# A hybrid diffusion backbone in fp32: each engine's instructions taken from a list schedule of the whole program

## The chip, the cores and the metric

The kernel runs on one core of a Trainium2 chip. The metric is device time in microseconds (us), the median of several runs. A core has five instruction streams that run side by side and each in its own order: TensorE (PE, matmuls; PEld is its weight load), VectorE (DVE), ScalarE (ACT), GpSimd (POOL) and SyncE (SP, which here only issues transfers). An instruction starts when its engine has started all those ahead of it and when the semaphores that it waits on have come; so the order inside each stream decides what stands behind a wait.

## The reference

The reference is a two-layer backbone over 256 context tokens and 512 latent tokens of width 1024, in fp32. Cut to what matters here, one layer is:

```python
p = modulate(x, sh1, sc1) @ w_in                     # norm(x) * (1 + sc) + sh, latent and context apart
ya = chunk_token_mlp(p[..., :512])                   # gelu, norm, 128x128 token mixing, gate
yb = gqa_mixer(p[..., 512:1152])                     # 6 query heads, 2 key heads, rotary, softmax
yc = deltanet_mixer(p[..., 1152:])                   # short conv, 6 heads, chunks of 64, both directions
x = layer_norm(ALPHA * x + g1 * (concat(ya, yb, yc) @ w_out))
m = jnp.square(jax.nn.relu(modulate(x, sh2, sc2) @ w_up)) @ w_down      # 1024 -> 4096 -> 1024
x = layer_norm(ALPHA * x + g2 * m)
```

The six modulation vectors of a layer come from `silu(c) @ mod_w`. In the second layer only the 512 latent tokens pass beyond the mixers. The gated DeltaNet is a recurrence: each chunk of 64 tokens solves a triangular system, and a 64x64 state per head passes from chunk to chunk.

## The kernel before, in words

**Arithmetic.** A large product is three matmuls of a rounded type, fp32r (`mm3`): each operand is split into a high part (a copy on ACT: `whi`, `xh`, `hh`) and a low part (a subtraction on DVE: `wlo`, `xl`, `hl`), and hi*hi, lo*hi and hi*lo are summed in PSUM. Small products and the recurrence are fp32 matmuls, which the trace records as two passes each.

**Memory.** Weights come in 512 KB pieces through `Feed` (L235): raw buffers `wraw`, filled by SP, and parts `whi` and `wlo`. PSUM is split into four slots of 512 columns (`mm`) and two of 1024 (`ax`).

**Stages**, each with its place in the profiled execution. Start (0 to 84 us): modulation of layer 0 (`modw` pieces times `cz`), norms and transposes of `xt`, first input projections (`w_ta`). Mixer input (`mix`, L711; 84 to 310 us): projections for gMLP, conv, q, k, v and z, and `dn_prep` of head pairs 0 and 1, whose triangular inverse is a chain of short DVE steps (`tm`, `Xx`), two DVE transposes (`PA`, `PB`) and 32x32 matmuls (`PB,M`; `PA,zs`). DeltaNet and attention (310 to 535): per head pair `dn_make` (`kv`, `rwu`), the state chain `dn_scan` (L1542: `S`, `rP`, `rQ`), and between them `attention` (L1056): scores into an `ax` slot (`akh,qs`), row maximum `anm` on DVE, exponential `ape` on ACT, scaling on DVE, transposes (`c_ident,ape`), copies `apT` on ACT and `att_out` (L1114), the product with the values (`apT,ava`), 64 columns of the array wide and 12 matmuls to a pair of heads. Output projection (535 to 605), then the MLP (`mlp`, L1711; 616 to 1180): eight groups of up units, each a pass over all tokens, and after each group the down product, token by token, each token in one `ax` slot whose sum DVE adds to `acc`. Layer 1 is the same with 4 token tiles in place of 6 behind the mixers: 1180 to 1424, 1424 to 1605, 1605 to 1675, 1675 to 2027. At the end each of four tokens has a norm (`acc`, `st`, `mv`, `rs`, `rstd`, twice `xt`) and a store.

**What sets the order.** `Flow` (L40) runs the stages as generators and picks, by a rough clock of its own, which one goes on next; its picks are the written order. Every instruction passes `_Engine.call`, so that all rows of the trace carry that line:

```python
def call(*args, **kw):
    self.flow.note(self.key, op, args, kw)
    return f(*args, **kw)          # L213
```

The framework then orders each engine by priority, which is the written order but for `prep`, started 300 places ahead (`AHEAD`). An accumulation group (the matmuls that sum into one slot) is written as one run, and so is each token of the down product and each pair's 12 products with the values.

Of the kernel before, what the change touches and what calls it, by code (L numbers as in the profile page):

```python
# [9 lines left out]
F32R = mybir.dt.float32r  # L10
# [3 lines left out]
PSUM = bass.MemoryType.PSUM  # L14
DRAM = bass.MemoryType.DRAM

P = 128
# [22 lines left out]
class Flow:  # L40
# [8 lines left out]
    def __init__(self, tc):  # L49
        self.tc = tc  # L50
        self.free = {}
        self.ready = {}
        self.done = {}
        self.live = []
        self.count = 0
        self.last = 0.0
        self.slots = {}
        self.spare = {}
        self.lent = {}
# [7 lines left out]
    @staticmethod  # L67
    def width(a):
        n = 1
        for s in a.shape[1:]:  # L70
            n *= s
        return n
# [150 lines left out]
            setattr(self, k, _Engine(flow, k, getattr(nc, k)))  # L223


def _tb(v):

    return 1 - v if v < 2 else 7 - v
# [62 lines left out]
class K:  # L291
    def __init__(self, ctx, tc, d, dump=None):
        self.tc = tc
        self.flow = Flow(tc)
        self.nc = _Core(tc.nc, self.flow)
        self.d = d
        self.dump = dump
        self.ctx = ctx
        self.open_ = []


    def open(self, name, side="left", space=None):
        kw = {} if space is None else {"space": space}
        cm = self.tc.tile_pool(name=name, bufs=1, side=side, reuse_waits="tile", **kw)
        p = cm.__enter__()
        self.open_.append((p, cm))
        return p

    def close(self, *pools):
        for p in pools:  # L310
            i = next(i for i, (q, _) in enumerate(self.open_) if q is p)
            self.open_.pop(i)[1].__exit__(None, None, None)

    def setup(self):
        nc, tc, ctx, d = self.nc, self.tc, self.ctx, self.d
# [348 lines left out]
def _body(ctx, tc, d, out, dump=None, stop=None):  # L664
    K_ = Kernel(ctx, tc, d, dump)
    K_.run(out, stop)
    for p, cm in reversed(K_.open_):
        cm.__exit__(None, None, None)

# [17 lines left out]
class Kernel(K):  # L687
# [784 lines left out]
    def dn_make(self, l, p, v, qkv, G, A, TT, r):  # L1472
# [5 lines left out]
        kds, ks, egc, be, E = G["kds"], G["ks"], G["egc"], G["be"], G["E"]  # L1478
        hs = slice(2 * p, 2 * p + 2)
        td = (v, _tb(v))  # L1480
        a0 = 0 if l == 0 else 2
        he = lambda a: a.rearrange("p t (h e) -> p t h e", e=HD)
# [59 lines left out]
    def dn_scan(self, l, p, v, A, r, S, o):  # L1542

        nc, sc = self.nc, self.dn
        need = l == 0 or v > 1
        a0 = 0 if l == 0 else 2
        td = (v, _tb(v))
        mm = nc.tensor.matmul
        halves = [_half(f) for f in range(2)]
# [405 lines left out]
```

## Time and profile before

| | |
|---|---|
| median of 3 runs | 2039.75 us (2034.57 to 2040.4) |
| profiled execution | 2039.17 us, span 2037.4 us, mean granted clock 0.95 |
| busy share | PE 91%, PEld 75%, DVE 63%, ACT 42%, POOL 14% |
| chain that ended last | PE 61%, DVE 18%, issue 7%, ACT 5%, POOL 4%, DMA 3% |

The busy share of PE counts matmuls that overlap in the pipeline, so a stage with a PE busy share of 80% can still have room; idle time of PE is stage length less busy time. The granted clock is 1 where TensorE runs at 2.4 GHz and 0.5 where it runs at 1.2 GHz; a stage's mean between the two tells how much of it ran at the lower level.

### The profile page before, as it was taken

The numbers are of one execution on the slowest core, as the hardware profiler recorded it, in microseconds if no ns is written. First come the engines' busy times: TensorE is split into PE (matmuls) and PEld (weight loads), VectorE is DVE, ScalarE is ACT, GpSimd is POOL, SyncE is SP. The second block draws the span as 40 slices with busy tenths as digits, with TensorE's granted clock in tenths as the row PEclk, the third lists the DMA queues.
The fourth block names the chain that finished last, engine by engine and source line by source line (L and its number), as shares of the span: only waits on it lengthen the run. The fifth ranks groups of instructions, "written<-read, shape, count | busy, mean of one in ns | idle before, by whom it ended". The sixth has DMA issues, their size and how long they took to land.

```text
span 2037.4 us, 35195 instructions
## 1 busy us (share of the span) xinstructions
PE 1859.2 (91%) x14496; PEld 1519.5 (75%) x14496; DVE 1284.2 (63%) x2165; ACT 854.5 (42%) x1607; POOL 279.2 (14%) x479
## 2 busy tenths in 40 slices
PE   6999887898898999999999989988778879999997
PEld 2778675566678878888888777877666668888886
DVE  4668786765587245464457776888785575544555
ACT  3434435456546322322232274443655545323331
POOL 1111215431021000000000111111522020000001
PEclk8989889989999999999999979987997989999999
DMA  8211015313326323242355242100000544322331
GB/s 284 93 58 50 27 37 175 120 31 118 107 96 226 99 83 115 83 155 74 113 165 185 84 147 89 62 29 21 27 27 6 189 164 136 103 83 83 114 104 52
DMA packets 74060, 204.44 MB, mean 100 GB/s; under 512 B 9730, under 2 KB 23938, under 8 KB 73900
## 3 DMA queue, kind: packets, MB, share of 16 engines
q1 hardware_dynamic: 62764, 184.51, 27.9%
q10 hardware_dynamic: 11136, 17.70, 2.3%
q8 instruction: 113, 1.85, 0.4%
q14 instruction: 47, 0.39, 0.1%
HBM read 184.38 MB, written 17.79 MB: 99 GB/s over the span
## 4 chain that ended last, share of the span: by engine, by line
PE 61%; DVE 18%; issue 7%; ACT 5%; POOL 4%; DMA 3%; SPq 0%; ACTq 0%; POOLq 0%; DVEq 0%
PE mm L213 37%; PE ax L213 25%; DVE cacc L213 2%; DVE Xx L213 2%; DVE tm L213 2%; DVE wlo L213 2%; POOL crn L213 2%; DVE M L213 1%; DMA wraw<-in_w_up 1%; POOL rs L213 1%; DVE anm L213 1%; ACT ape L213 1%; DVE st L213 1%; POOL arn L213 1%; ACT osq L213 1%
## 5 line engine op out<-in xcount | busy, mean ns | idle before, releaser
L213 ACT ACTIVATE whi<-wraw 128x1024 fp32r<-128x1024 f32 (+2 forms) x188 | 194.6, 1050 | 443.1 <-PE ax L213 287.7
L213 DVE TENSOR_TENSOR wlo<-wraw,whi 128x1024 fp32r<-128x1024 f32 (+2 forms) x188 | 226.6, 1212 | 236.5 <-ACT whi L213 235.7
L213 PE MATMUL mm<-x2xh,whi 128*128 128x256 f32 (+1 forms) x832 | 287.7, 346 | 12.3 <-ACT whi L213 11.2
L213 PE MATMUL mm<-x2xl,whi 128*128 128x256 f32 (+1 forms) x832 | 287.0, 345 | 0.0
L213 PE MATMUL mm<-x2xh,wlo 128*128 128x256 f32 (+1 forms) x832 | 285.4, 343 | 0.7 <-DVE wlo L213 0.7
L213 PE MATMUL ax<-whi,hh 128*128 128x512 f32 x640 | 251.4, 393 | 0.1
L213 PE MATMUL ax<-wlo,hh 128*128 128x512 f32 x640 | 250.2, 391 | 0.0
L213 PE MATMUL ax<-whi,hl 128*128 128x512 f32 x640 | 250.1, 391 | 0.0
L213 PEld LDWEIGHTS mm<-x2xh,whi 128*128 128x128 f32 x832 | 159.7, 192 | 34.6 <-ACT whi L213 12.0
L213 DVE TENSOR_TENSOR acc<-acc,ax 128x1024 f32<-128x1024 f32 x68 | 83.0, 1220 | 148.3 <-PE ax L213 148.2
L213 PEld LDWEIGHTS mm<-x2xh,wlo 128*128 128x128 f32 x832 | 159.0, 191 | 20.0 <-DVE wlo L213 1.1
L213 PEld LDWEIGHTS mm<-x2xl,whi 128*128 128x128 f32 x832 | 159.7, 192 | 17.5
L213 PEld LDWEIGHTS ax<-whi,hh 128*128 128x128 f32 x640 | 120.2, 188 | 29.6 <-ACT hh L213 5.6
L213 PEld LDWEIGHTS ax<-whi,hl 128*128 128x128 f32 x640 | 120.2, 188 | 27.3 <-DVE hl L213 2.9
L213 PEld LDWEIGHTS ax<-wlo,hh 128*128 128x128 f32 x640 | 120.3, 188 | 26.9 <-issue 2.6
L213 POOL TENSOR_SCALAR rs<-mv 128x1 f32<-128x1 f32 x52 | 33.1, 638 | 702.6 <-DVE mv L213 701.4
L213 DVE SCALAR_TENSOR_TENSOR acc<-modw,cz,acc 128x1024 f32<-128x1024 f32 x80 | 101.2, 1282 | 7.6 <-DMA acc<-in_mod_b 4.6
L213 ACT ACTIVATE rl<-mm 128x256 f32<-128x256 f32 (+1 forms) x104 | 50.7, 490 | 131.4 <-PE mm L213 131.4
L213 POOL MEMSET acc<- 128x1024 f32 x10 | 9.5, 955 | 468.9 <-PE mm L213 468.9
L213 DVE TENSOR_TENSOR hl<-rl,hh 128x768 fp32r<-128x768 f32 (+2 forms) x76 | 54.5, 717 | 29.7 <-ACT hh L213 29.7
L213 DVE TENSOR_REDUCE anm<-ax 128x1 f32<-128x768 f32 (+1 forms) x60 | 50.6, 848 | 33.3 <-PE ax L213 33.2
L213 DVE SCALAR_TENSOR_TENSOR cacc<-cb,cw,cacc 128x772 f32<-128x772 f32 (+1 forms) x72 | 70.0, 975 | 0.7 <-ACT cacc L213 0.2
(255 smaller groups left out, 4127.1 us busy)
## 6 DMA issues: line engine op xcount, KB each, us to landing
modw<-in_mod_w SPq DMA_DIRECT2D x80, 512.0 KB
wraw<-in_w_up SPq DMA_DIRECT2D x64, 512.0 KB
wraw<-in_w_down SPq DMA_DIRECT2D x64, 512.0 KB
wraw<-in_w_ch SPq DMA_DIRECT2D x22, 512.0 KB
modw<-in_mod_w SPq DMA_DIRECT2D x32, 256.0 KB
wraw<-in_w_out SPq DMA_DIRECT2D x16, 512.0 KB
x_d<-xt ACTq DMA_DIRECT2D x16, 512.0 KB
xt<-x_d SPq DMA_DIRECT2D x14, 512.0 KB
```

The source lines that it names most:

```text
L213: return f(*args, **kw)
```

## The change

After all instructions are written, a new class `Order` builds a graph of the whole program: which instruction reads or writes what another wrote (`graph`), which waits for a buffer of a pool to come free, and the order of first use of the buffers of a tag. `tail` gives each instruction the length of the longest chain of work from it to the end of the program. `schedule` then runs through the program with five engines and one transfer bus, always giving a free engine the ready instruction with the longest chain behind it, and `apply` fixes the resulting order of each engine with dependencies that carry no semaphore. The instructions are the same. Pools are wrapped so that their opening, closing and tiles are recorded (`Pools`, `_Pool`, not shown).

```diff
+class Order:
+    SAME, OTHER = 110.0, 220.0
...
+    def costs(self):
...
+            elif kind == "InstMatmult":
+                n = width(x.outs[0])
+                m = width(x.ins[1])
+                if x.ins[1].dtype == F32R:
+                    c = max(35.0 + 0.58 * m, 0.4175 * n + 13.0)
+                else:
+                    c = (1.0 if x.is_transpose else 2.0) * max(0.42 * m, 0.835 * n + 2.0)
+                o, l = x.outs[0].bass_ap, x.ins[1].bass_ap
+                self.cells[-1] = self.place(x)
...
+    def lag(self, i, j):
+        if i >= self.n or j >= self.n:
+            return 0.0
+        if self.moved[i]:
+            return 0.0
+        if self.eng[i] == self.eng[j]:
+            return 0.0 if self.cells[i] else self.SAME
+        return self.OTHER
...
+    def tail(self):
...
+        for i in reversed(order):
+            c = self.dur[i] + (2200.0 + self.moved[i] / 340.0 if self.moved[i] else 0.0) if i < self.n else 0.0
+            far[i] = c + max((far[j] + self.lag(i, j) for j in succ[i]), default=0.0)
+            if i < self.n:
+                far[i] = max([far[i]] + [far[j] + 1.0 for j in self.after[i]])
...
+    def schedule(self, key):
...
+        for _ in range(self.n):
+            best = None
+            for e in self.engines:
+                if avail[e]:
+                    t = free[e]
+                elif soon[e]:
+                    t = max(free[e], soon[e][0][0])
+                else:
+                    continue
+                if best is None or t < best[0]:
+                    best = (t, e)
+            t, e = best
+            while soon[e] and soon[e][0][0] <= t + 1.0:
+                r, i = heapq.heappop(soon[e])
+                heapq.heappush(avail[e], (key[i], i))
+            k, i = heapq.heappop(avail[e])
+            t = max(t, ready[i])
+            if self.cells[i]:
+                t = max([t] + [cell[c] for c in self.cells[i]])
+                for c in self.cells[i]:
+                    cell[c] = t + self.dur[i]
+                fin = t + self.dur[i]
+                free[e] = t + 7.0
+                if len(self.cells[i]) == 16:
+                    free[e] = fin
...
+    def apply(self):
+        far = self.tail()
+        out = self.schedule([-f for f in far])
+        dep = mybir.DependencyInfo(mybir.DependencyClass.NoSync, mybir.DependencyReason.DATA)
+        for e, seq in out.items():
+            for a, b in zip(seq, seq[1:]):
+                self.tc.add_manual_dep(self.ins[b], self.ins[a].name, dep)
...
 def _body(ctx, tc, d, out, dump=None, stop=None):
     K_ = Kernel(ctx, tc, d, dump)
     K_.run(out, stop)
+    Order(tc, K_.pools).apply()
```

The order that comes out stands near the written one: a matmul moves by 22 places of 11,078 on average, a DVE instruction by 7. Three places show what moves.

DVE at the end of layer 0's mixer input, where the DeltaNet begins: `PA` and `PB` close the triangular inverse of pair 1, `M` belongs to pair 2 and follows a transfer (`gc_d`), `zth` is the gate of z, `akl` the low part of the keys, and `kv` the first step of pair 0's `dn_make`. Before:

```order
L213 STREAM_TRANSPOSE PA<-Xx 128x32x32
L213 STREAM_TRANSPOSE PB<-Xx 128x32x32
L213 SCALAR_TENSOR_TENSOR zth<-zth,mm_69 128x384
L213 SCALAR_TENSOR_TENSOR zth<-zth,ng 128x384
L213 TENSOR_TENSOR M<-M,gc 128x768
L213 TENSOR_TENSOR M<-M,c_mask 128x768
L213 SCALAR_TENSOR_TENSOR zth<-zth,mm_66 128x384
L213 TENSOR_TENSOR akl<-akT,akh 64x256
L213 SCALAR_TENSOR_TENSOR zth<-zth,ng 128x384
L213 TENSOR_TENSOR akl<-akT,akh 64x256 x3
L213 TENSOR_TENSOR akl<-akT,akh 64x512 x3
L213 TENSOR_TENSOR kv<-qkv_991,ks 128x2x64 x2
```

Now:

```order
L213 TENSOR_TENSOR akl<-akT,akh 64x512
L213 TENSOR_TENSOR Xx<-Xx,tm 128x2x30
L213 TENSOR_TENSOR kv<-qkv_991,ks 128x2x64
L213 TENSOR_TENSOR tm<-Lx,Xx 128x31
L213 TENSOR_TENSOR kv<-qkv_991,ks 128x2x64
L213 TENSOR_TENSOR Xx<-Xx,tm 128x31
L213 TENSOR_TENSOR kv<-qkv_991,be 128x2x64
L213 STREAM_TRANSPOSE PA<-Xx 128x32x32
L213 STREAM_TRANSPOSE PB<-Xx 128x32x32
L213 TENSOR_TENSOR kv<-qkv_992,ks 128x2x64 x2
L213 TENSOR_TENSOR kv<-qkv_992,be 128x2x64
L213 TENSOR_TENSOR rP_2759<-mm_69,ei 128x256
```

The three `kv` of the first block stand among the last steps of the inverse and ahead of `PA` and `PB`, and `M` is no longer ahead of them. On PE the rest of pair 1's preparation (`PB,M`, `PA,zs`), which stood ahead of the last projection, now follows the first `kv,TT` and its successors.

PE in the last third of layer 0's attention, where the DeltaNet has ended; `mm` is a slot of 512 columns, `ax` one of 1024. Before:

```order
L213 MATMUL mm_69<-c_ident,ape 128x128 x4
L213 MATMUL mm_66<-c_ident,ape 128x128 x2
L213 MATMUL ax_71<-akh,qs 128x512
L213 MATMUL ax_71<-akl,qs 128x512
L213 MATMUL ax_71<-akh,qs 128x256
L213 MATMUL ax_71<-akl,qs 128x256
L213 MATMUL mm_68<-apT,ava 64x128 x11
L213 MATMUL mm_67<-c_ident,ape 128x128 x4
L213 MATMUL mm_69<-c_ident,ape 128x128 x2
```

Now:

```order
L213 MATMUL ax_70<-akh,qs 128x256
L213 MATMUL mm_68<-apT,ava 64x128 x2
L213 MATMUL ax_70<-akl,qs 128x256
L213 MATMUL mm_68<-apT,ava 64x128 x2
L213 MATMUL mm_67<-c_ident,ape 128x128
L213 MATMUL mm_68<-apT,ava 64x128 x2
L213 MATMUL mm_67<-c_ident,ape 128x128
L213 MATMUL mm_68<-apT,ava 64x128 x2
L213 MATMUL mm_67<-c_ident,ape 128x128
L213 MATMUL mm_68<-apT,ava 64x128 x2
L213 MATMUL mm_66<-c_ident,ape 128x128
L213 MATMUL mm_68<-apT,ava 64x128
```

The run of 12 products with the values is cut into pieces of one or two, and the transposes of the next heads, which stood behind it in runs of four and two, stand singly between the pieces; the scores of both following heads stand ahead.

DVE at the very end of the program, the last two tokens. Before:

```order
L213 TENSOR_TENSOR acc<-acc,ax_71 128x1024
L213 BN_STATS st<-acc 128x6 x2
L213 BN_AGGR mv<-st 128x2
L213 SCALAR_TENSOR_TENSOR xt<-acc,mv,lg 128x1024
L213 SCALAR_TENSOR_TENSOR xt<-xt,rstd,lb 128x1024
L213 TENSOR_TENSOR acc<-acc,ax_70 128x1024
L213 BN_STATS st<-acc 128x6 x2
L213 BN_AGGR mv<-st 128x2
L213 SCALAR_TENSOR_TENSOR xt<-acc,mv,lg 128x1024
L213 SCALAR_TENSOR_TENSOR xt<-xt,rstd,lb 128x1024
```

Now:

```order
L213 TENSOR_TENSOR acc<-acc,ax_71 128x1024
L213 TENSOR_TENSOR acc<-acc,ax_70 128x1024
L213 BN_STATS st<-acc 128x6 x4
L213 BN_AGGR mv<-st 128x2 x2
L213 SCALAR_TENSOR_TENSOR xt<-acc,mv,lg 128x1024 x2
L213 SCALAR_TENSOR_TENSOR xt<-xt,rstd,lb 128x1024 x2
```

The two tokens advance together. On PE it is the same in all down products: the two `ax` slots take one matmul each in turn, the two tokens end with neighbouring matmuls, and the next pair follows them; up units advance in twos as well. On SP, at the start, 18 `modw` pieces follow the first transfer `c_cT` at once, `c_ident`, `modb`, `c_sel` and `c_mask` come later, and the first `w_ta` pieces stand ahead of the last five `modw` and of the gMLP constants.

## Rows read from the trace of the kernel before

**Rows 1.** The page: busy time of the engines, and the chain that ended last.

```profile
PE 1859.2 (91%) x14496; PEld 1519.5 (75%) x14496; DVE 1284.2 (63%) x2165; ACT 854.5 (42%) x1607; POOL 279.2 (14%) x479
...
PE 61%; DVE 18%; issue 7%; ACT 5%; POOL 4%; DMA 3%; SPq 0%; ACTq 0%; POOLq 0%; DVEq 0%
```

**Rows 2.** Busy time by stage: us, PE, PEld, DVE, ACT, POOL, clock, DMA, GB/s.

```profile
84.00:310.00 226.00, 202.07 (x1491) 166.83 (x1489) 164.52 (x327) 89.01 (x141) 34.57 (x37) 0.91 0.14 45
310.00:535.00 225.00, 192.84 (x3280) 140.31 (x3280) 146.18 (x354) 128.75 (x364) 73.11 (x156) 0.93 0.33 108
616.00:1180.00 564.00, 557.58 (x2914) 471.81 (x2913) 309.72 (x306) 169.12 (x242) 23.27 (x28) 0.99 0.39 125
1180.00:1424.00 244.00, 214.47 (x1407) 182.48 (x1407) 189.96 (x403) 121.26 (x208) 40.66 (x52) 0.89 0.21 68
1424.00:1605.00 181.00, 146.29 (x2861) 118.93 (x2854) 124.92 (x301) 110.22 (x288) 60.93 (x132) 0.91 0.13 44
1675.00:2027.00 352.00, 351.09 (x1622) 291.06 (x1621) 182.47 (x179) 128.11 (x184) 6.13 (x8) 1.00 0.31 101
```

**Rows 3.** Timeline of SP: start, length, what it issued, at the start.

```profile
1.16 0.42 SPq L213 DMA_DIRECT2D c_ident<-in_ident  x1
...
3.82 9.89 SPq L213 DMA_DIRECT2D modw<-in_mod_w  x16
...
37.32 1.36 SPq L213 DMA_DIRECT2D wraw<-in_w_ta  x3
```

**Rows 4.** Timeline of PE: first input projection, idle before it in brackets.

```profile
46.20 0.40 PE L213 MATMUL mm<-whi,xh 128*128 128x280 f32 x1 [2.01 <-ACT whi L213]
```

**Rows 5.** What PE waited for, whole program: us, times, longest.

```profile
PE mm L213 <- DVE axn L213: 10.6, 3, 6.2
...
PE mm L213 <- issue: 2.8, 1, 2.8
```

**Rows 6.** Timeline of DVE where the DeltaNet of layer 0 begins.

```profile
309.24 0.96 DVE L213 TENSOR_TENSOR M<-M,gc 128x768 f32<-128x768 f32 x1 [5.24 <-DMA M<-gc_d]
...
316.61 0.80 DVE L213 TENSOR_TENSOR kv<-qkv,ks 128x128 f32<-128x128 f32 x2
```

**Rows 7.** Timeline of PE at the same place.

```profile
317.15 0.69 PE L213 MATMUL mm<-kv,TT 64*64 64x128 f32 x4 [8.13 <-DVE kv L213]
```

**Rows 8.** Timeline of PE, attention of layer 0, first stretch.

```profile
446.13 0.66 PE L213 MATMUL mm<-c_ident,ape 128*128 128x128 f32 x4
446.55 0.48 PE L213 MATMUL ax<-akh,qs 128*128 128x512 f32 x1
```

**Rows 9.** Timeline of PE, attention of layer 0, second stretch.

```profile
470.67 0.66 PE L213 MATMUL mm<-c_ident,ape 128*128 128x128 f32 x4
471.26 0.43 PE L213 MATMUL mm<-apT,ava 128*64 128x128 f32 x2
471.62 0.50 PE L213 MATMUL ax<-akh,qs 128*128 128x512 f32 x1
...
472.28 1.52 PE L213 MATMUL mm<-apT,ava 128*64 128x128 f32 x22
473.74 0.39 PE L213 MATMUL ax<-akh,qs 128*128 128x256 f32 x1
```

**Rows 10.** Timeline of DVE, a token of the down product, layer 0.

```profile
732.80 1.22 DVE L213 TENSOR_TENSOR acc<-acc,ax 128x1024 f32<-128x1024 f32 x1 [2.86 <-PE ax L213]
```

**Rows 11.** Timeline of DVE, first token of the last group, layer 0.

```profile
1144.00 1.23 DVE L213 TENSOR_TENSOR y<-ax,g 128x1024 f32<-128x1024 f32 x1 [4.04 <-PE ax L213]
```

**Rows 12.** Timeline of PE at the very end.

```profile
2026.74 0.39 PE L213 MATMUL ax<-whi,hl 128*128 128x512 f32 x1
```

**Rows 13.** Timeline of DVE at the very end.

```profile
2027.17 1.22 DVE L213 TENSOR_TENSOR acc<-acc,ax 128x1024 f32<-128x1024 f32 x1 [0.69 <-PE ax L213]
...
2029.99 1.28 DVE L213 SCALAR_TENSOR_TENSOR xt<-acc,mv,lg 128x1024 f32<-128x1024 f32 x1
2031.99 1.28 DVE L213 SCALAR_TENSOR_TENSOR xt<-xt,rstd,lb 128x1024 f32<-128x1024 f32 x1 [0.71 <-POOL rstd L213]
```

More of the change, by code (lines that the diff above doesn't have):

```diff
@@ new lines, with __init__, size, tile @@
+class Pools:
+    def __init__(self):
+        self.events = []
+class _Pool:
+    def __init__(self, pools, pool, side):
+        self.pools, self.pool, self.side, self.tags = pools, pool, side, {}
+        pools.events.append(("open", self))
+    def size(self):
+        return sum(b * n for b, n, _ in self.tags.values())
+    def tile(self, shape, dtype, tag=None, bufs=1, name=None):
+        kw = {} if tag is None else {"tag": tag}
+        t = self.pool.tile(shape, dtype, bufs=bufs, name=name, **kw)
+        tag = tag or name
+        n = 4 * math.prod(shape[1:])
+        n = -(-n // 32) * 32
+        b, k, names = self.tags.get(tag, (0, 0, []))
+        names.append(t.tensor.name if hasattr(t, "tensor") else t.name)
+        self.tags[tag] = max(b, n), max(k, bufs), names
+        return t
@@ L299, in __init__ @@
         self.open_ = []
+        self.pools = Pools()
     def open(self, name, side="left", space=None):
@@ L304, in open @@
         cm = self.tc.tile_pool(name=name, bufs=1, side=side, reuse_waits="tile", **kw)
-        p = cm.__enter__()
+        p = _Pool(self.pools, cm.__enter__(), side)
         self.open_.append((p, cm))
@@ L312, in close @@
             self.open_.pop(i)[1].__exit__(None, None, None)
+            self.pools.events.append(("close", p))
     def setup(self):
```

231 lines of the change are left out of this document (added).

## The prediction

> **What bounds the kernel now.** I read the page first, then the busy time by stage, then the waits of PE, then the timelines at the places that the new order touches. PE is busy for 91% of the span, and it makes up 61% of the chain that ended last, DVE 18% [rows 1]. The average hides two kinds of stage [rows 2]. In the two MLPs PE hardly stops: 557.6 of 564 us in layer 0 and 351.1 of 352 us in layer 1, at a granted clock of 0.99 and 1.00. An order can win nothing there; it can only lose. Elsewhere PE has holes: 23.9 us in the mixer input of layer 0 (226 less 202.07), 32.2 in its DeltaNet and attention, 29.5 and 34.7 in the same stages of layer 1, and the clock stands at 0.89 to 0.93. So the reader is to ask of each stage which hole a new order fills, and of the MLPs which cover it removes.
>
> The sum is made against the profiled execution, 2039.17 us, which stands 0.6 us under the median of the runs (2039.75).
>
> **Start.** SP spends 2.66 us on `c_ident`, `c_sel`, `c_mask` and `modb` ahead of the first `modw` (1.16 to 3.82), and issues `w_ta` only at 37.32 [rows 3]. Now `modw` goes first, and `w_ta` stands ahead of the last five `modw`, whose issue it delays by its own 1.36 us. The first projection then no longer waits for `whi` (2.01 us of idle ahead of 46.20 [rows 4]). 2.66 - 1.36 + 2.01 = 3.3: I take -3. If the last `modw` set the end of this stage alone, the bytes of `w_ta` now in front of them eat the gain (+1 at worst); at best the 2.01 and twice the 2.66 go, -7.
>
> **Mixer input, layer 0.** The two longest named holes are 6.2 us before the transposes of `axn` and 2.8 us after the gates, an "issue" row [rows 5]. The new order puts the last projections of q and k behind the first, and conv matmuls around the second. 9.0 us of the 23.9 are thus covered by work that was there anyway, but two thirds at most, since the DVE chain behind both (`tm`, `Xx` of pair 1) is stretched by what is put between its steps: -6, from 0 to -9.
>
> **Entry of the DeltaNet, layer 0.** DVE waits 5.24 us for the transfer of `M`, and `kv`, which needs nothing of it, is queued behind until 316.61 [rows 6]; PE stands 8.13 us ahead of `kv,TT` [rows 7]. In the new order `kv` is ahead of `PA`, and `kv,TT` follows the projections. The hole of 8.13 goes; next late is pair 1, whose `PA` and `PB` come behind three `kv` (0.40 us each) and some `akl`. -6, from 0 to -8.
>
> **DeltaNet and attention, both layers: the shape of the array.** The new order cuts the product with the values into pieces. Each of these matmuls has two records. Before, 22 records (11 matmuls) of `apT,ava` take 1.46 us to the start of the next instruction (472.28 to 473.74), and 2 records (one matmul) take 0.36 (471.26 to 471.62) [rows 9]. So 10 matmuls more cost 1.10, or 0.11 each, and leaving the 64-wide shape costs 0.25 whatever the length. Four transposes take 0.42 to the next instruction of the same shape [rows 8] and 0.59 to one of the 64-wide shape [rows 9]: entering costs 0.17. Counted over the two orders, steps from 128x64 to 128x128 go from 24 to 80 in layer 0 and from 10 to 39 in layer 1, the way back from 25 to 75 and from 12 to 33; all changes of shape from 171 to 309 and from 121 to 249. That is 85 x 0.25 = 21 us, 71 x 0.17 = 12 us, and for the other 110, which have no row as clean, 0 to 0.1 each; I take 4: 37 us more work for PE in stages where it now has 32 and 35 us of idle time. Hidden altogether it costs 0. Exposed at PE's share of the chain, 61%, it costs 23. Against that the state chain now goes first wherever it is ready, which no row prices. I take +10, from 0 to +37.
>
> The Trainium skill, page "TensorEngine Tiling (Array Packing)", section "Tiling Modes", says under its key properties that a change of tiling mode drains TensorE, a change of tile alone does not. The rows above agree as far as they go: the loss is at the change and not in the length of the run. By the rule each of the 266 added changes would pay, at 0.25 us 66 us in place of 37, and with the same share of it exposed the term would be 18 in place of 10.
>
> **The MLPs.** Before, tokens of the down product use the two `ax` slots in turn, so that each sum on DVE has a whole token of the other slot as its cover: one token of 18 matmuls lasts 2.86 + 1.22 = 4.08 us, 0.227 a matmul [rows 10]. Now two tokens end with neighbouring matmuls and the next one needs the same slot. From the last matmul's start to the sum's start are 0.43 us (2026.74 to 2027.17 [rows 12, 13]), the sum takes 1.22, and PE starts 0.14 after a DVE result (the first `kv` of two ends at 317.01, PE starts at 317.15 [rows 6, 7]): 1.79. At 22 such places in both MLPs the order leaves little cover, at most of them 8 matmuls, 1.82 us. It just fits, with nothing over; whatever DVE has in hand at that moment is paid in full. DVE is busy 55% and 52% of these stages [rows 2]; if it were always half through a sum, 22 x 0.61 = 13 us. Since the places are filled by a model that sees DVE's other work too, I take 0.1 each: +2, from 0 to +13.
>
> **End of the first MLP.** DVE's closing work begins at 1144.00, 4.04 us after it had nothing to do [rows 11], and it is what the next layer waits for. In pairs the first two tokens end 30 matmuls later than the first one did, 30 x 0.227 = 6.8; the transposes of the first tokens are pulled forward and give some of it back: +4, from 0 to +7.
>
> **Mixer input and DeltaNet, layer 1.** The same moves meet smaller holes: 29.5 us in many pieces, where I take -4 (0 to -15, half of them), and 34.7 us, where the whole early chain of pair 0 is now interleaved with the triangular inverse of pair 1: -8 (0 to -17). Both are shares of idle time that I chose near the 6 of 24 in layer 0, not sums of rows.
>
> **The end.** The last pair starts two matmuls after the one before it (0.45 of the 1.79 needed): +1.3. Then both tokens end together. One token's DVE work from the sum to the first `xt` is 4.10 us (2027.17 to 2031.27) and the second `xt` 1.28; its last `xt` ended at 2033.27, 6.10 after the start [rows 13]. Two tokens in a row are 2 x 4.10 + 2 x 1.28 = 10.8, which hides the wait for `rstd` but not the other token: +4.5. Together +6, from +3 to +7, and nothing covers it.
>
> **Sum.** -3 - 6 - 6 + 10 + 2 + 4 - 4 - 8 + 6 = -5. 2039.2 - 5 = 2034.2, in the scale of the median 2034.8; I say 2034.
>
> **Rivals.** First, nothing to speak of happens: the instructions move by 22 places of 11,078, the holes that are filled come back at the end of the stage, because the same chain of DVE and PE steps ends it. For it speaks that every stage still hands over to the next through one chain; against it that the 8.13 us hole is a matter of queueing alone [rows 6, 7]. 2038.
>
> Second, the clock. The stage rows show 0.91, 0.93, 0.89 and 0.91 [rows 2]; with two levels, 1 and 0.5, that is 18%, 14%, 22% and 18% of these stages at 1.2 GHz, 41 + 32 + 54 + 33 = 159 us. If filled holes turn half of that to 2.4 GHz, its work takes half the time, 40 us less on PE, and at 61% of the chain 24: 2034 - 24 = 2010. Against it: the pieces of the product with the values add stops of their own.
>
> Third, slower. The mechanism is PE's changes of shape in the stages of DeltaNet and attention, the 266 added ones. In the last third of layer 0's attention nothing but attention is left, so the pieces stand on the chain there and in all places where PE is what the stage waits for. At 61% exposed the term is 23 in place of 10, 2047; at all of it 37, 2061. I give it 2055. It decides from 22 us exposed on, where the sum is +7. The MLPs' missing cover would add to it, up to 11.
>
> **How the numbers follow.** A measurement of this kernel tells about 0.3%, 6 us, from no change: faster is below 2033.6, slower above 2045.9. My forecast has 0.42; its own range is 2020 to 2047, of which 0.20 lies on the faster side, 0.16 within, 0.06 slower. The clock has 0.16, nearly all faster. Nothing happens: 0.14, of it 0.11 within. Shapes: 0.28, all slower. Together faster 0.37, within 0.28, slower 0.35. Each end leaves out about 1 in 10: 1998, below the clock's price, and 2064, just above the shapes fully exposed.
>
> **What would show it.** In the profile after: the first projection earlier than 46 us by about 3; no hole of 8 us before `kv,TT`; in the last attention stretch runs of `apT,ava` of 2 and 4 records with about 0.3 us between the starts of the next shapes, and this stretch longer, not shorter; in the MLPs PE busy still above 99% (a few short waits for `acc` would be the missing cover; 0.5 us at each place would prove me too low by 9); the end, from the start of PE's last matmul to the end of the span, some 15 us in place of 10.7. I am wrong if the DeltaNet stages get shorter by more than 20 us, or if the MLPs lose more than 10.

## The result: slower, and the profile after

The changed kernel takes 2068.73 us (median of 4 runs, 2067.76 to 2069.97) against 2040.08 for the kernel before in the same comparison: 1.0146 times as long, 95% interval 1.0127 to 1.0165. The profiled execution took 2068.96 us, its span is 2067.1, its mean granted clock 0.947. The forecast was 2034, the range 1998 to 2064: wrong in direction, and just outside the range.

The page's busy line, which answers to [rows 1]:

```profile
PE 1906.5 (92%) x14496; PEld 1531.4 (74%) x14496; DVE 1283.5 (62%) x2165; ACT 845.8 (41%) x1605; POOL 291.5 (14%) x479
```

PE has the same 14,496 records and is busy 47 us longer, while its idle time fell from 178 us to 161. So the order did fill holes; but the same matmuls took longer. The stages, cut where the same work begins and ends as in [rows 2]:

```profile
84.00:288.00 204.00, 191.83 (x1312) 159.97 (x1310) 164.81 (x318) 86.39 (x136) 42.30 (x47) 0.96 0.19 61
288.00:535.00 247.00, 220.98 (x3492) 150.66 (x3492) 149.39 (x363) 135.32 (x375) 67.89 (x145) 0.93 0.29 93
620.00:1181.00 561.00, 558.23 (x2912) 471.81 (x2913) 297.52 (x290) 160.47 (x235) 20.30 (x23) 0.99 0.36 121
1187.00:1409.00 222.00, 203.56 (x1372) 173.23 (x1371) 173.96 (x363) 111.75 (x191) 51.26 (x58) 0.90 0.22 70
1409.00:1630.00 221.00, 187.85 (x2902) 141.03 (x2902) 139.74 (x343) 113.08 (x292) 61.01 (x128) 0.83 0.11 36
1696.00:2053.00 357.00, 353.95 (x1640) 294.56 (x1640) 182.32 (x180) 129.24 (x191) 4.53 (x6) 0.99 0.31 100
```

Both mixer inputs got about 20 us shorter (226 to 204, 244 to 222), both stages of DeltaNet and attention longer (225 to 247, 181 to 221), the last one at a clock of 0.83 in place of 0.91. A stage table can move time between neighbours, so here is when the same instructions ran, in us, before, after, and in the kernels of the experiments that matter most (e1: each pair's product with the values whole; e5: that, and changes of shape charged for; e10: the charge alone):

| stretch, from and to | before | after | e1 | e5 | e10 |
|---|---|---|---|---|---|
| start to first projection | 46.2 | 47.5 | 48.6 | 49.5 | 49.1 |
| to the first `kv`, layer 0 | 270.4 | 246.7 | 244.3 | 242.9 | 243.3 |
| to the last `S` | 154.4 | 153.7 | 157.8 | 153.9 | 156.9 |
| to the first product of `yh` (attention's tail) | 67.4 | 87.2 | 66.4 | 65.1 | 64.0 |
| to the first up product | 83.5 | 84.7 | 83.9 | 84.4 | 84.3 |
| MLP, to the last down product | 557.5 | 561.4 | 562.7 | 560.0 | 560.0 |
| layer 1: first projection to first `kv` | 240.4 | 222.1 | 223.2 | 220.4 | 220.2 |
| to the last `S` (DeltaNet) | 163.5 | 192.7 | 179.8 | 164.3 | 166.5 |
| to the last product with the values (`apT,ava`) | 20.3 | 24.2 | 23.3 | 21.2 | 19.1 |
| to the first up product (output projection) | 60.8 | 70.7 | 71.7 | 71.0 | 74.0 |
| MLP, to PE's last matmul | 358.6 | 356.4 | 355.8 | 356.0 | 356.2 |
| to the end of the span | 10.3 | 14.4 | 14.4 | 14.1 | 14.2 |

Between the two rows of layer 0's MLP and layer 1's first projection lie 4.1 us before and 5.4 after. Three rows of this table lose 59 us together: attention's tail of layer 0 (+19.8), the DeltaNet of layer 1 (+29.2) and the output projection of layer 1 (+9.9). The mixers gain 42 (23.7 and 18.3).

**Attention's tail.** PE's timeline of after, where before had runs of 22 records [rows 9]:

```profile
486.08 0.44 PE L213 MATMUL mm<-apT,ava 128*64 128x128 f32 x4
486.45 0.33 PE L213 MATMUL mm<-c_ident,ape 128*128 128x128 f32 x1
486.70 0.44 PE L213 MATMUL mm<-apT,ava 128*64 128x128 f32 x4
```

Two products (two records each) and one transpose take 0.62 us from start to start. Uninterrupted they take 2 x 0.11 + 0.11 = 0.33 [rows 8, 9]. Nearly half of this piece is two changes of shape, 0.29, with PE recorded as busy throughout: the cost can't be seen as idle time. It shows when equal stretches are set side by side. Attention's tail and layer 1's DeltaNet, from before:

```profile
471.00:538.40 67.40, 55.42 (x469) 43.01 (x467) 38.92 (x71) 46.08 (x119) 3.35 (x4) 0.97 0.35 118
1424.00:1587.40 163.40, 132.97 (x2744) 108.64 (x2738) 115.64 (x284) 98.45 (x248) 58.22 (x128) 0.90 0.08 24
```

The same two stretches of after:

```profile
447.90:535.10 87.20, 75.59 (x464) 46.41 (x464) 37.11 (x69) 45.23 (x118) 3.53 (x4) 0.90 0.27 91
1408.70:1601.40 192.70, 168.75 (x2754) 127.99 (x2754) 129.57 (x325) 98.36 (x247) 57.50 (x124) 0.82 0.06 19
```

For nearly the same number of PE records, busy time grew by 20.2 and 35.8 us, 56 together. Idle time fell from 12.0 to 11.6 and from 30.4 to 24.0. So in these two stretches only 6.9 of 56 us were hidden in holes. The trace counts 140 changes of shape in the tail in place of 45, and 228 in layer 1's DeltaNet in place of 114. In the tail DVE and ACT do no more than before: nothing is there to hide behind. In that DeltaNet the clock fell too: at 0.90 of 163.4 us, 33 us ran at 1.2 GHz, at 0.82 of 192.7 it is 69 us. Work at 1.2 GHz takes at most twice as long, so of the 29 us at most 18 are the clock's and at least 11 are not; in the tail (4 and 17 us at 1.2 GHz) at most 7 of 20.

The DeltaNet of layer 0 (first `kv` to last `S`) went the other way. Before, and after:

```profile
316.60:471.00 154.40, 138.94 (x2835) 98.58 (x2836) 100.80 (x274) 77.98 (x235) 63.16 (x142) 0.92 0.30 96
294.20:447.90 153.70, 144.60 (x3026) 103.75 (x3026) 106.97 (x280) 85.71 (x247) 64.36 (x141) 0.97 0.29 94
```

It holds 170 changes in place of 125 and 191 more records, work that stood ahead of it before, and yet it is no longer: PE's idle time took up the 5.7 us, and the clock rose. So the added changes were not exposed everywhere, and here more of them did not go with a lower clock.

**DeltaNet of layer 1.** PE's timeline of after, at 2.4 GHz and then, from about 1451 on, at 1.2 GHz:

```profile
1440.26 0.33 PE L213 MATMUL mm<-c_ident,ape 128*128 128x128 f32 x1
1440.52 0.33 PE L213 MATMUL mm<-A,rwu 64*64 64x64 f32 x4
1440.69 0.28 PE L213 MATMUL mm<-id,qd 64*64 64x64 f32 x4
1440.90 0.33 PE L213 MATMUL mm<-c_ident,ape 128*128 128x128 f32 x1
...
1445.02 0.63 PE L213 MATMUL mm<-rwu,A 64*64 64x64 f32 x16
1445.48 0.40 PE L213 MATMUL mm<-S,rQ 64*64 64x64 f32 x8
...
1451.21 0.48 PE L213 MATMUL mm<-A,rwu 64*64 64x64 f32 x4
1451.48 0.42 PE L213 MATMUL mm<-id,qd 64*64 64x64 f32 x4
1451.83 0.31 PE L213 MATMUL ax<-PB,M 32*32 32x32 f32 x2
1452.07 0.48 PE L213 MATMUL mm<-A,rwu 64*64 64x64 f32 x4
...
1454.20 2.12 PE L213 MATMUL ax<-PB,M 32*32 32x32 f32 x70
1456.25 0.69 PE L213 MATMUL mm<-S,rP 64*64 64x64 f32 x8
...
1457.28 1.12 PE L213 MATMUL mm<-rwu,A 64*64 64x64 f32 x16
1458.19 0.64 PE L213 MATMUL mm<-S,rQ 64*64 64x64 f32 x8
```

A transpose alone between 64x64 pieces takes 0.26 (1440.26 to 1440.52) in place of 0.11; the four records ahead of the next one take 0.21 (1440.69 to 1440.90), where 16 in a row take 0.46, or 0.115 for four: 0.24 for two changes, 0.12 each. At 1.2 GHz a cycle with 32x32 takes 0.86 (1451.21 to 1452.07); eight 64x64 records at 0.057 (16 in 0.91) and two 32x32 at 0.029 (70 in 2.05) make 0.51, so 0.17 for each change. These are the "other 110" changes of the prediction, which it priced at 0.04.

The clock of that stretch and the next, after:

```profile
1451.00:1482.00 31.00, 29.59 (x411) 21.60 (x408) 14.93 (x33) 16.27 (x45) 9.05 (x16) 0.50 0.08 27
1483.00:1514.00 31.00, 31.00 (x511) 23.07 (x507) 23.52 (x67) 16.35 (x37) 10.78 (x27) 1.00 0.09 25
```

The first ran at 1.2 GHz, with PE recorded as busy for 95% of it, the next at 2.4 GHz. Before the fall stands a wait of PE for `PB`, 2.75 us up to 1449.85.

**Output projection of layer 1.** PE's timeline of after at its first product:

```profile
1634.39 1.22 PE L213 MATMUL mm<-whi,yh 128*128 128x512 f32 x2 [8.76 <-ACT whi L213]
```

ACT's timeline of after, where the weight's high part stands behind a `yh` and its own transfer:

```profile
1629.25 0.52 ACT L213 ACTIVATE yh<-y 128x384 fp32r<-128x384 f32 x1 [3.31 <-DMA y<-y_d]
1633.28 1.06 ACT L213 ACTIVATE whi<-wraw 128x1024 fp32r<-128x1024 f32 x1 [3.52 <-DMA wraw<-in_w_out]
```

And SP's:

```profile
1592.67 25.98 SPq L213 DMA_DIRECT2D y<-y_d  x4
...
1625.34 7.38 SPq L213 DMA_DIRECT2D wraw<-in_w_out  x3
```

Three weights are issued on SP behind four transfers of `y` that wait 26 us for the attention's output, as the last products with the values run (they end at 1625.6). Before, they were issued at 1592.68, 15 us ahead of that end. PE then waits 8.76 us. That is 7.0 of the 9.9: from the last product with the values to the first product of `yh` it is 8.8 us in place of 1.8. The products of `yh` themselves take 2.2 less, and from the last of them to the first up product it is 12.6 in place of 7.4. There PE waits for `v` four times, the longest:

```profile
1693.46 1.12 PE L213 MATMUL mm<-c_ident,xn 128*128 128x128 f32 x4 [3.27 <-ACT v L213]
```

ACT copies `v` in small groups with the MLP's `whi` (1.04 to 1.07 each) between them. No kernel was made for this part; with the written key, below, it takes 8.7.

**What the order filled.** PE's waits over the whole program, after:

```profile
PE mm L213 <- ACT v L213: 16.6, 12, 3.3
PE ax L213 <- ACT ape L213: 14.2, 12, 5.7
...
PE mm L213 <- DVE axn L213: 4.9, 4, 2.3
...
PE mm L213 <- DVE kv L213: 1.9, 2, 1.1
```

`axn` fell from 10.6 to 4.9 [rows 5], `kv` from 8.13 [rows 7] to 1.9. Larger are `ape`, from 7.4, and `v`, from 2.1. At the entry of layer 0's DeltaNet DVE now starts `kv` between the steps of `tm` and `Xx`, and `kv,TT` starts at 294.63 in place of 317.15:

```profile
294.20 0.28 DVE L213 TENSOR_TENSOR kv<-qkv,ks 128x128 f32<-128x128 f32 x1
294.40 0.18 DVE L213 TENSOR_TENSOR tm<-Lx,Xx 128x31 f32<-128x31 f32 x1
```

**The end.** PE's timeline of after, for [rows 12]:

```profile
2038.76 0.50 PE L213 MATMUL ax<-whi,hh 128*128 128x512 f32 x1 [1.09 <-DVE acc L213]
...
2052.05 0.61 PE L213 MATMUL ax<-whi,hl 128*128 128x512 f32 x2
```

The last pair waits 1.09 us for its slot. DVE's, for [rows 13], with both sums in one row:

```profile
2052.47 2.35 DVE L213 TENSOR_TENSOR acc<-acc,ax 128x1024 f32<-128x1024 f32 x2 [4.43 <-PE ax L213]
```

### The profile page after: what moved, and what is told of

It is laid out like the page before. It is cut to its first block, busy times and chain, and to the rows that moved or that the text cites. A ratio compares the mean times of both kernels' runs of the same rounds, so it can differ in the third digit from the quotient of the medians.

```text
span 2067.1 us, 35248 instructions
## 1 busy us (share of the span) xinstructions
PE 1906.5 (92%) x14496; PEld 1531.4 (74%) x14496; DVE 1283.5 (62%) x2165; ACT 845.8 (41%) x1605; POOL 291.5 (14%) x479
## 5 line engine op out<-in xcount | busy, mean ns | idle before, releaser
L213 PE MATMUL mm<-x2xh,whi 128*128 128x512 f32 (+1 forms) x832 | 232.6, 345 | 9.1 <-ACT whi L213 5.4
L213 PE MATMUL mm<-x2xh,wlo 128*128 128x512 f32 (+1 forms) x832 | 230.1, 343 | 0.0
L213 PE MATMUL mm<-x2xl,whi 128*128 128x512 f32 (+1 forms) x832 | 228.7, 344 | 0.0
L213 PE MATMUL ax<-whi,hh 128*128 128x512 f32 x640 | 208.9, 393 | 2.9 <-DVE y L213 1.7
L213 PE MATMUL ax<-wlo,hh 128*128 128x512 f32 x640 | 206.5, 390 | 0.0
L213 PE MATMUL ax<-whi,hl 128*128 128x512 f32 x640 | 203.9, 390 | 0.0
L213 PEld LDWEIGHTS mm<-x2xl,whi 128*128 128x128 f32 x832 | 149.3, 192 | 19.2
L213 PEld LDWEIGHTS ax<-wlo,hh 128*128 128x128 f32 x640 | 119.0, 188 | 23.3
L213 ACT ACTIVATE rl<-mm 128x512 f32<-128x512 f32 (+1 forms) x104 | 49.3, 490 | 125.1 <-PE mm L213 122.9
L213 PE MATMUL mm<-apT,ava 128*64 128x128 f32 x624 | 80.5, 318 | 4.6 <-ACT apT L213 3.4
L213 PE MATMUL mm<-c_ident,ape 128*128 128x128 f32 x312 | 71.3, 320 | 3.1 <-DVE ape L213 2.9
```

## The experiments

The theory: the new order pays for PE's changes of shape with nothing to hide them. Its rivals: the loss is in waits, in SP's order, or in down products that end in pairs. All kernels are the changed one with `Order` edited. Changes of shape below are counted in the trace over four stretches, the mixer input and the DeltaNet with attention of both layers: 348 before, 627 after.

### Products with the values whole

```diff
+            if any(nm.startswith("apT") for nm in names):   # a pair's 12 products: one group
+                runs[-1].append(i); self.group[i] = runs[-1][0]
...                                                           # the first waits for all their inputs
+                same = [(key[j], j) for q, j in avail[e] + soon[e] if run and self.group[j] == run]
+                if same:
+                    k, i = min(same)
```

> As the changed kernel (2068.7 us), but the scheduler keeps the 12 products with the values of a pair of heads in one run on PE: it starts them when all copies apT are there and goes on with them until the last. Changes of shape in the two DeltaNet stages fall from 304 and 252 to 169 and 175 (169 and 121 before). Theory 1, changes of shape (my term of +10 was too small; the attention of layer 0 after the last state step went from 74 to 95 us up to the end of the output projection's start): the pieces are fully exposed, and half of the clock loss follows from them; about 25 to 35 us come back, 2034 to 2044, and the stretch from the last S of layer 0 to the first yh falls from 87 to under 72 us. Theory 2, the attention is long because the DeltaNet now ends 23 us earlier and leaves the attention alone, bound by its own chain of anm, ape, apT: the stretch stays above 80 us and the whole at 2060 or more.

2035.20 us, 0.9970 of before (0.9956 to 0.9985): 33.5 us less than after. 409 changes. PE in the tail:

```profile
481.26 2.01 PE L213 MATMUL mm<-apT,ava 128*64 128x128 f32 x24
```

Twelve products in one run, 21 changes left in the tail, and it takes 66.4 us, as theory 1 had it. Those 20 us are the cut products. Of the DeltaNet's 29 only 13 came back, at a clock of 0.86.

### The written order as the key, cut and whole

```diff
-        out = self.schedule([-f for f in far])
+        out = self.schedule(list(range(self.m)))
```

> As the changed kernel, but the list schedule picks the ready instruction that was written first, not the one with the longest chain behind it. Shapes change 319 and 232 times in the DeltaNet stages. Theory 1, the scheduler takes whatever is ready and so cuts runs whatever its key is: 2060 to 2080, with the attention of layer 0 as long as in the changed kernel. Rival, the key by longest chain is what interleaves: 2045 or less.

2056.07 us, 1.0076 (1.0055 to 1.0098), between the two theories. Without the chains as key the program is 13 us shorter than after, with about as many changes (551 against 556 in the two stages of DeltaNet and attention), but a tail of 75.9 us and an output projection of 64.3. The DeltaNet of layer 1 is the plainest case: 220 changes against 228, and 178.8 us at a clock of 0.89 against 192.7 at 0.82. So the number of changes alone doesn't decide. With the products whole as well:

> As e1 (products whole), but the ready instruction written first is taken, not the one with the longest chain. Theory 1, the 33 us that e1 gave back are those of the cut products and come back under either key: 2056 less 21 to 30 is 2026 to 2035. Rival, the written key's advantage of 12 us in e4 was only that it cut less: then here it is slower than e1, 2040 or more.

2033.83 us, 0.9969 (0.9956 to 0.9981): keeping the products whole saves 22 us here, as theory 1 had it.

### Two that missed

SP left to the framework, and every started group of the rounded type finished before another one starts (so that tokens of the down product don't pair up):

```diff
+            if e in (mybir.EngineType.SP,):
+                continue
```

> As the changed kernel, but SP's order is left to the framework; the other four engines keep the list schedule. In layer 1 all but four of the loads of y stand before the first w_out piece as before, so the loads are not moved much. Theory 1, SP's queue: w_out of layer 1 waits behind a load of y that waits for the last attention output (8.8 us of PE idle before whi); here it stands behind four loads of y still, so only what the framework moves elsewhere shows, 2060 to 2069. Rival: the loads of w_out wait for their buffers and not for the queue; then the order of SP changes nothing at all, 2068 within 4.

2082.17 us, 1.0211 (1.0178 to 1.0243), slower than either theory said: the first projection comes at 54.2 in place of 47.5, and what after loses is not won back by the framework's order of SP.

```diff
+            if x.ins[1].dtype == F32R and self.group[i] is None:
+                self.group[i] = x.outs[0].bass_ap.tensor.name
```

> As the changed kernel, but a started accumulation group of fp32r matmuls is finished before another starts, so tokens of the down product and up units go one after the other again. Theory 1, pairs of tokens: the end after PE's last matmul falls from 14.6 to under 11 us and the end of the first MLP gets 5 us shorter; the MLPs' bodies stay as they are (they lost 1 us); 2059 to 2064. Rival, missing cover in the MLPs: the bodies of the two MLPs get shorter by 3 us or more each. Rival, neither: 2068 within 4.

2082.55 us, 1.0204 (1.0172 to 1.0236). The end took 10.2 us, as expected, but the second MLP 361.7, layer 0's output projection 88.9, and one wait for `xn` alone 12.8: with a group held to, PE waits where it went on with another before. So this run puts no price on the pairs; by the table above both MLPs, the end of the first and the end of the program are 7 us longer together, whatever the cause.

### A price for a change of shape

```diff
+                k, i = min((q + (5000.0 if self.shape[j] != shape else 0.0), j) for q, j in avail[e])
...
+                t += 200.0 if self.shape[i] != shape else 0.0
```

A matmul of another shape goes first only if the chain behind it is 5 us longer. With whole products:

> As e1 (products with the values whole, 2035 us), and the scheduler also weighs the shape: a ready PE instruction of another shape of the array than the last must have a chain longer by 5 us to be taken, and is charged 0.2 us. Changes of shape fall from 169 and 175 to 142 and 128 (169 and 121 in the kernel before). What is open after e1: the DeltaNet of layer 1, from the first kv to the last S, takes 180 us there and 164 before, though the attention is whole. Theory 1, the other changes of shape (64x64 against 128x128): it falls to 172 or less and the total to about 2025. Theory 2, the order of work in it (pair 0's early chain among pair 1's inverse, begun 32 us earlier): it stays at 177 or more, and the total within 5 of 2035.

2013.05 us, 0.9868 (0.9851 to 0.9885), 315 changes, 12 us under what theory 1 said. Tail and DeltaNet of layer 1:

```profile
446.30:511.40 65.10, 53.08 (x466) 42.01 (x464) 37.09 (x66) 43.62 (x117) 3.53 (x4) 0.97 0.36 122
1382.00:1546.30 164.30, 135.40 (x2768) 111.48 (x2770) 135.42 (x344) 101.23 (x253) 55.70 (x123) 0.91 0.08 24
```

PE's busy time and the clock are those of before; the gain of the mixers stays. The charge alone, the products free to be cut:

> As the changed kernel, with e5's charge for a change of shape but without the rule that keeps the products whole: 178 and 159 changes of shape in the DeltaNet stages (304 and 252 in the changed kernel, 142 and 128 in e5). Theory, it is the number of changes that costs, wherever they stand: e5 lies 56 us under the changed kernel for 286 changes fewer, 0.19 us each; 219 fewer give 43 us, 2026, plus or minus 6. Rival, only the whole products matter: 2045 or more.

2019.47 us, 0.9895 (0.9873 to 0.9917), 383 changes, just under the 2020 to 2032 expected: a price does nearly all of what the rule for the products does, and also what that rule doesn't do in the DeltaNet. And four times the chain demanded, with whole products (20000 for 5000; the 0.2 us charged stay):

> As e5 with a charge of 20 us of chain in place of 5: 119 and 94 changes, fewer than before the change (169 and 121). Theory 1, still 0.19 us for each of the 57 fewer: 2002. Theory 2, below some number the chain of the DeltaNet waits for its place: 2010 or more.

2069.66 us, 1.0140 (1.0114 to 1.0166), 248 changes, the fewest, and as slow as after. PE's waits in it:

```profile
PE mm L213 <- DVE axn L213: 21.2, 6, 8.2
...
PE mm L213 <- DVE S L213: 9.9, 12, 1.9
```

Now the chains wait for PE's shape (`axn` 4.9 in after, `S` 4.0). So the demand on the chain can be too high; the charge of 0.2 us without any demand was not tried.

### More changes

```diff
+                k, i = min((q + (-1000.0 if self.shape[j] != shape else 0.0), j) for q, j in avail[e])
```

The other shape is preferred, with products cut or whole:

> The suspected cost made larger: as the changed kernel, but an instruction of another shape than the last is preferred by 1 us of chain. 411 and 388 changes of shape in the DeltaNet stages (304 and 252 in the changed kernel). Theory, each change costs PE what the rows show wherever it stands, and the stages pay it: 243 more at 0.16 to 0.22 us (e1, e10 against the changed kernel) give 39 to 53 us, 2108 to 2122. Rival, what e1, e5 and e10 gave back came from the better order of the attention and the DeltaNet and not from the number of changes: within 12 of 2069.

> As e1 (products whole, 169 and 175 changes, 2035 us), with the same preference for another shape in all other instructions: 214 and 225 changes. Theory, the same price for the changes between 64x64 and 128x128: 95 more give 15 to 21 us, 2050 to 2056. Rival, only the products with the values matter: 2035 within 5.

2189.07 us, 1.0713 (1.0691 to 1.0734), 1058 changes; and 2110.73 us, 1.0347 (1.0317 to 1.0378), 689 changes. Both are slower than expected, in part because the expectations counted only the two stages of DeltaNet and attention, and the mixer inputs got changes too (about 240 of the 1058, before some 55 of the 348); together they take 49 us more than in after, in either kernel. Tail and DeltaNet of the first:

```profile
498.90:594.80 95.90, 85.72 (x464) 50.03 (x463) 36.79 (x68) 43.95 (x116) 2.95 (x4) 0.90 0.24 83
1492.30:1729.70 237.40, 216.59 (x2764) 155.11 (x2766) 131.57 (x326) 101.74 (x253) 58.14 (x126) 0.76 0.05 16
```

The same 2,764 records keep PE busy for 217 us where before they took 133, at a clock of 0.76. By pairs of kernels one change costs 33.5 / 218 = 0.15 us (after and e1), 49.3 / 244 = 0.20 (after and e10), 120.3 / 431 = 0.28 (e13 and after) and 75.5 / 280 = 0.27 (e14 and e1), the clock's part and what waits behind them included.

### The end

The last four tokens one after another on PE, with whole products:

```diff
+        last = set(mms[-120:])
+            if i in last:
+                self.group[i] = x.outs[0].bass_ap.tensor.name
```

> As e1, but the four tokens of the very last down product go one after the other. Theory 1, pairs at the end: from PE's last matmul to the end of the span 14.4 us become 10 to 11, total 2031. Rival (e3 lost 14 us by finishing every group first): PE waits for the ax slots between these tokens and the gain is eaten, 2035.

2031.44 us, 0.9949 (0.9933 to 0.9966), the time that theory 1 gave, but not by its mechanism: from PE's last matmul to the end it is still 13.7 us, and the interval overlaps that of e1. DVE:

```profile
2010.72 1.22 DVE L213 TENSOR_TENSOR acc<-acc,ax 128x1024 f32<-128x1024 f32 x1 [2.92 <-PE ax L213]
2011.98 2.47 DVE L213 BATCH_NORM_STATS2 st<-acc 128x6 f32<-128x512 f32 x4
```

The sums come one by one, but DVE's fixed order still has both norms behind the second sum.

### The weights of the output projection

With whole products, layer 1's first three pieces of `w_out` are put ahead of the last four `y` transfers on SP; then `whi` and `wlo` ahead of `yh` and `yl` on ACT and DVE as well; then that in the charged kernel (e12); then six pieces in place of three, with whole products (e15) and in the charged kernel (e16):

```diff
+        w = [i for i in sp if src(i) == "in_w_out"][8:11]      # e15, e16: [8:14]
+        at = sp.index(ys[0]); sp[at:at] = w                    # e6: SP alone
...
+            moves.append((e, sorted(mine, key=out[e].index), yr[-1]))   # e9 on: ACT and DVE too
```

> As e1, but on SP the first three pieces of w_out of layer 1 stand ahead of the load of y that waits for the last attention output, as before the change. Theory 1, SP's queue: from the last apT product to the first up matmul of layer 1 are 72 us in e1 and 61 before; this falls to 62 to 66, total about 2028. Rival, the pieces wait for their buffers wherever they stand: 70 or more, total as e1.

2035.47 us, 0.9972 (0.9959 to 0.9984), the rival's number for another reason; no gain: the weights come early, but `whi` stands behind a `yh` that waits for its `y`.

> As e6 (products whole, w_out of layer 1 early on SP), and on ACT and DVE the first three whi and wlo of w_out stand ahead of the yh and yl that wait for the last attention output. e6 brought the loads 15 us forward and PE's wait for whi stayed at 8.8 us. Theory, the same order stood on ACT too: whi waited 6.9 us behind yh, which waits for a store and a load of y. Then here the stretch from the last apT product to the first up matmul of layer 1 falls from 72 to 65 or less, total 2026 to 2030. Rival, PE itself needs the late y first: 70 or more, total 2035.

2032.77 us, 0.9964 (0.9949 to 0.9979). PE:

```profile
1592.09 1.22 PE L213 MATMUL mm<-whi,yh 128*128 128x512 f32 x2 [2.93 <-ACT whi L213]
...
1605.17 1.22 PE L213 MATMUL mm<-whi,yh 128*128 128x512 f32 x2 [3.56 <-ACT whi L213]
```

The wait of 8 us is 2.9 now, and the next three pieces cost 3.56: the stretch is 71.3 us, and neither the 65 nor the 2026 to 2030 of the theory came.

> e5 and e9 together. If the two costs are independent, e5's 2013 less what e9 gives back against e1 (6 to 9): 2004 to 2007. Rival, with the shorter DeltaNet the loads come early enough anyway: 2012.

2013.86 us, 0.9867 (0.9846 to 0.9887): no gain over e5, nearer the rival's 2012 than the 2004 to 2007 expected.

> The kernel that keeps each product with the values in one run, with the next six pieces of the output projection's weights in layer 1 (in place of three) ahead on all three streams: their transfers on SP in front of the y transfers, their whi on ACT and wlo on DVE in front of yh and yl. Theory (a queue: the ten microseconds lost in this stretch are transfers of weights behind transfers of y, and parts of weights behind parts of y; with three pieces the wait only moved to the next ones): the wait of 3.6 us at 1605 goes as well, the stretch from the last apT to the first up product falls from 71 to 66-68 us, and the kernel takes 2026 to 2030. Rival (PE is held by the values v and by the layer's own norm chain, the weights only hide it): the whi wait goes, waits for v, br or mv grow in its place, the stretch stays at 70 to 72 and the kernel at 2032 to 2036.

> The same six pieces ahead in the kernel with the charge for a change of shape. Theory (queue): 2013 falls by 3 to 5, to 2008 to 2010. Rival: 2012 to 2015, as with three pieces.

2026.93 us, 0.9937 (0.9913 to 0.9961), and 2008.11 us, 0.9839 (0.9820 to 0.9857), both as the queue theory had them. PE of e15:

```profile
1589.61 1.22 PE L213 MATMUL mm<-whi,yh 128*128 128x512 f32 x2 [3.18 <-ACT whi L213]
1599.64 0.73 PE L213 MATMUL mm<-whi,yh 128*128 128x512 f32 x2 [0.46 <-ACT whi L213]
```

The second wait is 0.46, the first 3.18; in e16 the first is 1.82, as long as before the change. The stretch takes 67.7 us and 67.2 in e16, against 71.7 and 71.0: 4 of the 10 us are this queue. What is left is mainly the 12.6 us ahead of the first up product, the same in both. As a whole e15 is 8 us faster than e1; the other 4 lie outside this stretch. The last, 2008 us, beats both kernels: 32 us under before.

## Why the prediction was wrong

**The step that failed is "DeltaNet and attention, both layers: the shape of the array", taken as +10.** The mechanism was the right one, and the third rival's; the term was mis-sized. Pricing the shapes in the changed kernel's scheduler, and nothing else (e10), gives back 49 us, what the clock and the waits add included; with whole products (e5) 56. Even the upper end of the term, 37, was too low for that. Three things were wrong in it. The exposed share, above all: PE's share of the chain over the whole program, 61%, and a discount on it, stood for places where the trace showed only PE and short waits; in the two stretches that got longer 6.9 of 56 us were hidden. Only in layer 0's DeltaNet did the holes take up what was added. The prices: the "other" 110 changes were taken at 0.04 and cost 0.12 to 0.17 in the rows above, 13 to 19 us in place of 4. The rest were taken too high for pieces of two products: that leaving the 64-wide shape costs 0.25 "whatever the length" doesn't hold, for one product takes 0.36 [rows 9] and two take 0.37 (486.08 to 486.45), and the pair of changes measured 0.29 in place of 0.42. So the 156 come to 23 to 33 us and all 266, an estimate from these rows, to 36 to 52. And the clock: the second rival let it only rise, but in layer 1's DeltaNet 69 us ran at 1.2 GHz in place of 33. The Trainium skill, page "TensorEngine Tiling (Array Packing)", section "Tiling Modes", has any change of tiling mode drain TensorE; the 0.12 to 0.17 for the changes that my term let nearly pass agree with it.

**Mixer input and entry, layer 0** (-6 and -6): right in kind, half in size. From the first projection to the first `kv` it is 23.7 us less. The wait for `axn` shrank and the 8.13 us hole went, as told.

**Mixer input, layer 1** (-4): 18.3 less, past the lower end of -15. **DeltaNet of layer 1** (-8): 29 more with the shapes in it. In e5 it is 0.8 more than before, so the gain of 8 isn't there either.

**What was not in it**: layer 1's output projection, +9.9. SP's queue was followed at the start alone; the order of the second `w_out`, behind the `y` transfers, could have been read as well.

**Start** (-3): +1.3. The first projection waits 1.56 us for `v`, and PE's waits for `modw` went from 7.4 to 9.9: no gain was there.

**MLPs and pairs** (+2, +4, +6): about right. The first MLP and its end took 3.9 and 1.3 more (5.2 for 6), the second 2.2 less; the end 4.1 more (15.1 from the start of the last matmuls, 10.6 before; some 15 was told). The 1.09 us for `acc` at the last pair was told as 1.3.

Split by e10, the change reads: all but the shapes -21 (e10 against before), the shapes +49 (after against e10). That these add up to the measured 28.7 is by construction; what it tells is that the other terms, -15 together, came out near, by misses that cancel, and that the range failed through one term, which was given a discount without a row for it. Both of the stated conditions for being wrong (DeltaNet stages much shorter, MLPs much longer) stayed out; what came was the last attention stretch in pieces and longer, as told, by 20 us.

**Open.** How much of the loss in the DeltaNet of layer 1 is the clock and how much the changes themselves (at most 18 of 29 and at least 11). After and e4, with nearly as many changes there, lie 14 us apart, at a clock of 0.82 and 0.89. Why e1, with 26 more changes than e10, is 16 us slower: of the 24 us between the two profiled executions 13.3 lie in the DeltaNet of layer 1 (179.8 against 166.5), at a clock of 0.86 against 0.90. And the 5 us between layer 1's last output product and its first up product, where only the rows were read. What makes the clock fall is open as well.

## What to carry to other kernels

A scheduler that orders TensorE by the length of chains alone will cut runs of one shape, so give its model a price for each change: with none the kernel was 29 us over before, with 0.2 us charged, near the measured price, and 5 us of chain demanded 21 to 28 under it, with 20 us demanded again 29 over. When work is added inside an engine's busy stretches, count it as exposed unless a row shows that engine waiting for something which the added work doesn't delay. After a reordering, walk every transfer queue past each stage's boundary: a load that stands behind a load which waits is as late as that one.

## What the runs showed of the hardware

A change of shape of the array costs time beyond the 64-wide products too: 0.12 us between 64x64 and 128x128 at 2.4 GHz, 0.17 between 64x64 and 32x32 at 1.2 GHz, and the profile counts it as PE's busy time. A 64-wide piece of one product and one of two take the same, 0.36 and 0.37 us up to the next instruction of another shape.

In the DeltaNet of layer 1 the granted clock was 0.91 (e5), 0.90 (before), 0.86 (e1), 0.82 (after) and 0.76 (e13), nearly in the order of the changes made there. Other stretches don't follow that order: 0.85 with 89 changes in e11, the fewest of all, 0.89 with 220 in e4, and in layer 0's DeltaNet 0.92 with 125 changes before and 0.97 with 170 after. So no run shows that changes of shape lower the clock.
